# The down-projection of a two-layer encoder in two groups of channel pairs, with every sum on VectorE

## The chip, the cores and the metric

The kernel runs on one core of a Trainium2 chip. A core has TensorE (PE: matmuls; PEld: its weight loads), VectorE (DVE), ScalarE (ACT), GpSimd (POOL) and SyncE (SP, which issues the transfers here), each with an instruction queue of its own that it works through in order. They share the on-chip memory SBUF; matmuls add up in PSUM banks. The metric is the device time of one execution in microseconds, the median of several runs. Beside the runs one execution was recorded by the profiler; its rows are shown below.

## The reference, cut to what matters

Two layers, each an attention mix and a gated MLP. The change lies in the second matmul of the MLP, `@ w_down`, and in the normalisation and residual sum behind it:

```python
def conv_gated_mlp(h, w_up, conv_w, conv_b, w_down):
    u = h @ w_up
    ...                      # depthwise convolution of width 3 over the tokens: c
    gate, val = jnp.split(c, 2, axis=-1)
    return (jax.nn.gelu(gate, approximate=True) * val) @ w_down     # 1024 x 2816 times 2816 x 1024
...
    h = rms_norm(x, ffn_pre_gain[l])
    y = conv_gated_mlp(h, w_up[l], conv_w[l], conv_b[l], w_down[l])
    x = x + rms_norm(y, ffn_post_gain[l])                           # the input of the next layer, or the output
```

All is float32 at the interface.

## The kernel before

A float32 matmul is made of three (`mm3`, lines 255 to 257): each operand is cast to a rounded high half (hi) and a remainder (lo), and the products hi x hi, hi x lo and lo x hi are summed.

`gated` (first MLP matmul) works over 22 chunks j of 128 channels. It writes each gated chunk to a DRAM buffer, `self.gate[j]`. Its weights rotate over buffers (`slot`), some of which are slices of a shared place, "more".

`down` (second matmul) takes the 22 chunks as 11 pairs. For each pair it does a 2 x 2 block product with seven half-size products for eight (P1 to P7, in the order P2, P1, P5, P6, P3, P7, P4). One product of one pair is four token tiles of three matmuls, 12 matmuls of 128x512. A pair's eight pieces of 128x512 (four of the gated chunks, four of `w_down`) are loaded into a place of SBUF, `r`, whose pieces are numbered 0 to 7. `prep` makes the operands of a product: sums or differences of pieces (L1509), the cast of both operands to hi on ACT (L1528, named dhP), and the subtraction that gives lo on DVE (L1529, dlP). hi and lo rotate over 12 buffers ("whl", "raw", "rg"), so six products can be prepared ahead at most.

The pairs come in groups. `places` lists the places that each group's pairs use: 0 to 3 are the shared places (`share`), "fx" is one more place in a pool that is opened when the gated stage's buffers are done. All pairs of a group go through P2, then all through P1, and so on, in blocks of two pairs for each token tile. When a product of a group is complete, `add` brings it from PSUM into y (rows named yfK, yfQ, yfV): in group 0 the first piece of each y is an ACT copy, the others are sums on DVE (L1582). One-bank results go through the banks "ob", "pb" and others, two-bank results (named dx) through `ps2`.

The order on all engines comes from `self.at(t, f)`: f is due at time t (`st` = 2.73 is one product), and `emit` calls all of them sorted by t. A `prep` is due `DL` products ahead of its product. Pieces of later groups are loaded `DD` products ahead, or as soon as the place's last use is over (`free`).

`tail(t, T)` finishes a token tile: load the residual row xf, square and reciprocal root (ACT, POOL), multiply by the gain (`leave`, L303, on DVE or POOL), add into xf (L309), store. In layer 0 it also normalises for the next layer and transposes the row through PSUM (`split`, L274, pt_f; each half is cast by ACT at L275 and subtracted by DVE at L276).

Of the kernel before, what the change touches and what calls it, by code (L numbers as in the profile page):

```python
# [44 lines left out]
def r32(ap):  # L45
# [25 lines left out]
    DL=4, DD=12, DA=-0.02, DW=-10, DX=7.6, EM=1.5, EX=4.59, ES=5.89)  # L71
# [3 lines left out]
class Kernel:  # L75
# [1184 lines left out]
    def gated(self, l, ops, rows):  # L1260
# [5 lines left out]
        with tc.tile_pool(name=f"fu{l}", bufs=1, reuse_waits="tile") as pool:  # L1266
# [20 lines left out]
            def slot(name):  # L1287
                x = slots[n[0] % len(slots)]
                n[0] += 1
                if isinstance(x, str):  # L1290
                    return self.wp.tile([128, D], F32R, tag=x, name=name, bufs=slots.count(x))
                return extra["more"][:, x]

            def weights(j):
# [7 lines left out]
                q = self.wp.tile([128, NK, 128], F32, tag="qs", name=f"sums{l}_{j}")  # L1302

# [167 lines left out]
    def down(self, l, x_src, x_dst):  # L1471
# [7 lines left out]
        places = [(1, 2, 3), ("fx", 0, 1, 2, 3), ("fx", 0, 1)]  # L1479
        operands = dict(P1=(2, 6), P2=(0, 4), P3=(0, 5), P4=(1, 4), P5=None, P6=(2, 6), P7=(3, 7))  # L1480
# [23 lines left out]
        def prep(n, nm, p, tags):  # L1504

            r, tag = pairs[p]["r"], f"{nm}{l}_{p}"

            def tt(eng, out, a, b, op=ALU.subtract):
                eng.tensor_tensor(out=out, in0=a, in1=b, op=op)  # L1509

            if nm == "P5":
                q = pairs[p]["q"] = x["pool"].tile([128, 2, 512], F32, tag="q", name=f"q{tag}", bufs=5)
                tt(nc.vector, q[:, 0], r[:, 3], r[:, 1], ALU.add)
                tt(nc.vector, q[:, 1], r[:, 7], r[:, 6])
            if nm == "P6":
                q = pairs[p]["q"]
                tt(nc.gpsimd, r[:, 3::4], r[:, 2:6:3], r[:, 3::4])
                tt(nc.vector, r[:, 2], q[:, 0], r[:, 2])
                tt(nc.vector, r[:, 6], r[:, 5], q[:, 1])
            if nm == "P5":  # L1520
                src = pairs[p]["q"]
            else:
                a, b = operands[nm]
                src = r[:, a:b + 1:b - a]
            hi, lo = (x["pool" if t in ("rg", "q") else "wp"].tile([128, 2, 512], F32R, tag=t, name=f"d{e}{tag}",
                                                                 bufs=dict(whl=6, raw=2, rg=4, q=5)[t])
                      for e, t in zip("hl", tags))
            nc.scalar.copy(hi, src)  # L1528
# [35 lines left out]
        def add(nm, t, g):  # L1564
# [19 lines left out]
        gain, nh, pool_ = [], [], []  # L1584
# [4 lines left out]
        def tail(t, T):  # L1589
# [61 lines left out]
        for g, pl in enumerate(places):  # L1651
# [3 lines left out]
            for m, nm in enumerate(order):  # L1655
# [3 lines left out]
                if g == 2 and nm in ("P3", "P4"):  # L1659
                    blocks = [list(range(n))]  # L1660
                for b, ks in enumerate(blocks):
                    final = b == len(blocks) - 1
                    for k in ks:
                        tags = [slots[i % 12] for i in (2 * s, 2 * s + 1)]
                        if g == 2 and nm == "P7":
                            tags = [("rg", "rg"), ("q", "q"), ("q", "q")][k]
                        if g == 2 and nm == "P4":
                            tags = ("whl", "whl") if k == 2 else ("rg", "rg")
                        t = (s - P["DL"]) * st
                        self.at(t, lambda s=s, nm=nm, p=p0 + k, tags=tags: prep(s, nm, p, tags))  # L1670
# [118 lines left out]
```

## Time and profile before

| | |
|---|---|
| median of 3 runs | 2734.23 us (2732.19 to 2738.07) |
| the profiled execution | 2732.83 us |
| its span, first to last instruction | 2731.1 us |
| mean granted clock of TensorE | 0.984 of full speed |
| busy: PE / DVE / ACT / POOL | 2569.6 / 2173.0 / 1465.5 / 937.8 us |
| the same as shares of the span | 94% / 80% / 54% / 34% |
| down-projection, layer 0 | 1131.46 to 1361.3, then transposes to 1393.5 |
| down-projection, layer 1 | 2488.0 to 2716.9, then the last tiles to 2731.1 |

Shares are averages over stages that differ. The windows below cut the down-projection into stretches: a stretch in which PE is busy all the time runs at PE's own pace, and one where PE is busy for less than its length waits for something. A row of windows has the stretch, its length, the busy time of PE, PEld, DVE, ACT and POOL with the number of instructions, the granted TensorE clock, the busy share of the DMA engines and their GB/s. The clock is the granted TensorE clock: 1.00 is the upper of its two levels (2.4 GHz), 0.5 the lower (1.2 GHz), and numbers between are mixtures over the stretch. A timeline row has the start, the length and the engine, and in brackets how long the engine was idle before and for what.

### The profile page before, as it was taken

The numbers are of one execution on the slowest core, as the hardware profiler recorded it, in microseconds if no ns is written. First come the engines' busy times: TensorE is split into PE (matmuls) and PEld (weight loads), VectorE is DVE, ScalarE is ACT, GpSimd is POOL, SyncE is SP. The second block draws the span as 40 slices with busy tenths as digits, with TensorE's granted clock in tenths as the row PEclk, the third lists the DMA queues.
The fourth block names the chain that finished last, engine by engine and source line by source line (L and its number), as shares of the span: only waits on it lengthen the run. The fifth ranks groups of instructions, "written<-read, shape, count | busy, mean of one in ns | idle before, by whom it ended". The sixth has DMA issues, their size and how long they took to land. (4 is left out here: it accounts for less than half of the span.)

```text
span 2731.1 us, 40409 instructions
## 1 busy us (share of the span) xinstructions
PE 2569.6 (94%) x14533; PEld 2208.2 (81%) x14533; DVE 2173.0 (80%) x3117; ACT 1465.5 (54%) x2704; POOL 937.8 (34%) x808
## 2 busy tenths in 40 slices
PE   8999999996899999989989999999968999998997
PEld 7999888885788888777789998888757888886876
DVE  5347899989878878797864568999897888878978
ACT  5247677666544444443553467776655444454433
POOL 1343212264333434241233442113733333332413
PEclk9999999999999999999999999999989999999999
DMA  6343412234222222622252434122432222216222
GB/s 194 101 128 88 106 49 69 57 90 148 78 70 93 77 77 78 212 89 93 94 161 85 125 96 92 48 70 62 105 123 81 82 84 79 83 65 223 77 93 100
DMA packets 316916, 268.02 MB, mean 98 GB/s; under 512 B 104763, under 2 KB 262571, under 8 KB 316715
## 3 DMA queue, kind: packets, MB, share of 16 engines
q1 hardware_dynamic: 316714, 265.43, 32.4%
q8 instruction: 114, 1.87, 0.3%
q14 instruction: 88, 0.71, 0.1%
HBM read 183.30 MB, written 69.48 MB: 93 GB/s over the span
## 5 line engine op out<-in xcount | busy, mean ns | idle before, releaser
L1305 POOL TENSOR_TENSOR sums<-loads 128x512 f32<-128x512 f32 x84 | 169.8, 2021 | 153.1 <-DMA loads<-in_w_up 67.2
L1528 ACT CAST dhP<-rows 128x1024 fp32r<-128x1024 f32 x108 | 110.7, 1051 | 171.8 <-PE dx L257 63.9
L1529 DVE TENSOR_TENSOR dlP<-rows,dhP 128x1024 fp32r<-128x1024 f32 x108 | 160.6, 1513 | 35.8 <-ACT dhP L1528 35.7
L1305 POOL TENSOR_TENSOR loads<-loads,sums 128x512 f32<-128x512 f32 x42 | 57.8, 1377 | 371.2 <-DVE wgl L1315 229.7
L1509 POOL TENSOR_TENSOR rows<-rows 128x1024 f32<-128x1024 f32 x36 | 109.4, 3044 | 169.8 <-DVE qP L1509 42.8
L256 PE MATMUL dx<-dlP,dhP 128*128 128x512 f32 x328 | 130.4, 398 | 12.8 <-DVE dlP L1529 12.8
L255 PE MATMUL dx<-dhP 128*128 128x512 f32 x328 | 130.2, 397 | 9.5 <-ACT dhP L1528 5.4
L257 PE MATMUL dx<-dhP,dlP 128*128 128x512 f32 x328 | 129.6, 395 | 0.0
L1188 ACT CAST PTh_b<-pt_b 128x512 fp32r<-128x512 f32 x128 | 74.9, 588 | 57.9 <-PE pt_b L1183 56.9
L1373 DVE SCALAR_TENSOR_TENSOR c<-ug,cw,c 128x1023 f32<-128x1023 f32 x44 | 56.8, 1290 | 56.2 <-ACT c L1372 56.2
L1372 ACT ACTIVATE c<-ug,cw 128x1024 f32<-128x1024 f32 x44 | 54.7, 1243 | 85.7 <-DMA gate<-c 82.7
L255 PE MATMUL pb_mix<-whi_wa,h 128*128 128x256 f32 x320 | 100.0, 313 | 0.1
L255 PE MATMUL ux<-fT,wqh 128*128 128x512 f32 (+1 forms) x256 | 96.7, 378 | 1.3 <-ACT fT L275 1.3
L256 PE MATMUL ux<-fT,wqh 128*128 128x512 f32 (+1 forms) x256 | 96.5, 377 | 0.0
L257 PE MATMUL ux<-fT,wql 128*128 128x512 f32 (+1 forms) x256 | 96.3, 376 | 0.0
L1415 ACT ACTIVATE c<-c 128x1024 f32<-128x1024 f32 x44 | 46.7, 1062 | 86.5 <-DVE c L1375 86.5
L1193 DVE TENSOR_TENSOR PTl_c<-pt_c,PTh_c 128x512 fp32r<-128x512 f32 x128 | 85.5, 682 | 8.5 <-ACT PTh_c L1188 7.9
L1193 DVE TENSOR_TENSOR PTl_b<-pt_b,PTh_b 128x512 fp32r<-128x512 f32 x128 | 87.0, 683 | 6.2 <-ACT PTh_b L1188 5.4
L1028 PE MATMUL s_b<-rK,rQ 128*128 128x512 f32 x256 | 91.5, 414 | 0.4 <-ACT P_b L1105 0.4
L1188 ACT CAST PTh_c<-pt_c 128x512 fp32r<-128x512 f32 x128 | 74.5, 587 | 32.1 <-PE pt_c L1183 30.4
L256 PE MATMUL pb_mix<-wlo_wa,h 128*128 128x256 f32 x320 | 90.3, 282 | 0.0
L257 PE MATMUL pb_mix<-whi_wa,h 128*128 128x256 f32 x320 | 90.3, 282 | 0.0
(613 smaller groups left out, 9716.2 us busy)
## 6 DMA issues: line engine op xcount, KB each, us to landing
loads<-in_w_up SPq DMA_DIRECT2D x84, 512.0 KB
gate<-c SPq DMA_DIRECT2D x44, 512.0 KB
rows<-gate SPq DMA_DIRECT2D x72, 256.0 KB
rows<-in_w_down SPq DMA_DIRECT2D x72, 256.0 KB
z<-z SPq DMA_DIRECT2D x28, 512.0 KB
rK<-rK SPq DMA_DIRECT2D x48, 256.0 KB
xs<-xo SPq DMA_DIRECT2D x16, 512.0 KB
xf<-xs SPq DMA_DIRECT2D x16, 512.0 KB
```

The source lines that it names most:

```text
L255: nc.tensor.matmul(out, ah, bh, start=start and i == 0, stop=False, **flags)
L256: nc.tensor.matmul(out, ah, bl, start=False, stop=False, **flags)
L257: last = nc.tensor.matmul(out, al, bh, start=False, stop=stop and i == n - 1, **flags)
L1028: nc.tensor.matmul(out[:, c:c + w], Q[:, qt * 128:(qt + 1) * 128], K[:, k0 + c:k0 + c + w], start=i == 0, stop=i == len(ops) - 1)
L1188: nc.scalar.copy(x["sp"][0][:np, :n], x["pt"][:np, :n])
L1193: nc.vector.tensor_tensor(out=x["sp"][1][:np, :n], in0=x["pt"][:np, :n], in1=r32(x["sp"][0][:np, :n]), op=ALU.subtract)
L1305: nc.gpsimd.tensor_tensor(out=out, in0=a, in1=b, op=op)
L1372: nc.scalar.activation(c, u, AF.Identity, bias=b, scale=w1)
L1373: nc.vector.scalar_tensor_tensor(out=c[:, 1:], in0=u[:, :S - 1], scalar=w0, in1=c[:, 1:], op0=ALU.mult, op1=ALU.add)
L1509: eng.tensor_tensor(out=out, in0=a, in1=b, op=op)
L1528: nc.scalar.copy(hi, src)
L1529: nc.vector.tensor_tensor(out=lo, in0=src, in1=r32(hi), op=ALU.subtract)
```

## The change

Two groups, of 5 and 6 pairs, replace three of 3, 5 and 3. A second extra place "fy" joins "fx". The operands of all seven products are formed in place in `r` by DVE alone, a sum when its product comes up (P5, P6, P3, P7) or behind P1's subtraction; the copies "q" and POOL's sums are gone. Group 0's first two products put hi and lo into place 0, which group 0 leaves free (`first`); the last five P4 put them into places whose pairs are done (`dead`).

```diff
-    DL=4, DD=12, DA=-0.02, DW=-10, DX=7.6, EM=1.5, EX=4.59, ES=5.89)
+    DL=3, DD=14, DG=(0, 2), DA=-0.02, DW=-10, DX=7.6, EM=1.5, EX=4.59, ES=5.89)
...
-        places = [(1, 2, 3), ("fx", 0, 1, 2, 3), ("fx", 0, 1)]
-        operands = dict(P1=(2, 6), P2=(0, 4), P3=(0, 5), P4=(1, 4), P5=None, P6=(2, 6), P7=(3, 7))
+        places = [(1, 2, 3, "fx", "fy"), (0, 1, 2, 3, "fx", "fy")]
+        operands = dict(P1=(2, 6), P2=(0, 4), P3=(0, 5), P4=(1, 4), P5=(3, 6), P6=(3, 6), P7=(2, 7))
...
+        def tt(out, a, b, op=ALU.subtract):
+            nc.vector.tensor_tensor(out=out, in0=a, in1=b, op=op)
+
+        def prep(s, nm, p, where):
 
             r, tag = pairs[p]["r"], f"{nm}{l}_{p}"
-
-            def tt(eng, out, a, b, op=ALU.subtract):
-                eng.tensor_tensor(out=out, in0=a, in1=b, op=op)
-
             if nm == "P5":
-                q = pairs[p]["q"] = x["pool"].tile([128, 2, 512], F32, tag="q", name=f"q{tag}", bufs=5)
-                tt(nc.vector, q[:, 0], r[:, 3], r[:, 1], ALU.add)
-                tt(nc.vector, q[:, 1], r[:, 7], r[:, 6])
+                tt(r[:, 3], r[:, 3], r[:, 1], ALU.add)
             if nm == "P6":
-                q = pairs[p]["q"]
-                tt(nc.gpsimd, r[:, 3::4], r[:, 2:6:3], r[:, 3::4])
-                tt(nc.vector, r[:, 2], q[:, 0], r[:, 2])
-                tt(nc.vector, r[:, 6], r[:, 5], q[:, 1])
-            if nm == "P5":
-                src = pairs[p]["q"]
+                tt(r[:, 3:7:3], r[:, 1:6:4], r[:, 2:7:4])
+            if nm == "P3":
+                tt(r[:, 0:5:4], r[:, 0:5:4], r[:, 3:7:3])
+            if nm == "P7":
+                tt(r[:, 7], r[:, 5], r[:, 7])
+            a, b = operands[nm]
+            src = r[:, a:b + 1:b - a]
+            if where is None:
+                hi, lo = ((self.wp if t != "rg" else x["pool"]).tile(
+                    [128, 2, 512], F32R, tag=t, name=f"d{e}{tag}", bufs=dict(whl=6, raw=2, rg=4)[t])
+                    for e, t in zip("hl", (slots[i % 12] for i in (2 * s, 2 * s + 1))))
             else:
-                a, b = operands[nm]
-                src = r[:, a:b + 1:b - a]
-            hi, lo = (x["pool" if t in ("rg", "q") else "wp"].tile([128, 2, 512], F32R, tag=t, name=f"d{e}{tag}",
-                                                                 bufs=dict(whl=6, raw=2, rg=4, q=5)[t])
-                      for e, t in zip("hl", tags))
+                hi, lo = where()
             nc.scalar.copy(hi, src)
             nc.vector.tensor_tensor(out=lo, in0=src, in1=r32(hi), op=ALU.subtract)
             ring[nm, p] = hi, lo
-            if nm == "P6":
-                tt(nc.gpsimd, r[:, 0::4], r[:, 0::4], r[:, 2::4])
+            if nm == "P1":
+                tt(r[:, 2:7:4], r[:, 2:8:5], r[:, 3:7:3])
+        def first(n):
+
+            if "first" not in x:
+                x["first"] = self.share(0, F32R, f"first{l}", (8, 512))
+            return [x["first"][:, 4 * n + e:4 * n + e + 2] for e in (0, 2)]
+
+        def dead(i, n):
+
+            if ("late", i) not in x:
+                x["late", i] = self.share(i, F32R, f"late{l}_{i}", (8, 512)) if i != "fx" else x["pool"].tile(
+                    [128, 8, 512], F32R, tag=i, name=f"late{l}_{i}")
+            return [x["late", i][:, 4 * n + e:4 * n + e + 2] for e in (0, 2)]
```

The P4 of group 1 goes in two blocks of three pairs, in layer 0 it adds onto banks of the P7 before it, and the transposes of tiles 0 to 3 come at due times of their own. All residual rows use three buffers, "z". The loads of group 0 have a new order: place 1 first, "fx" and "fy" from the moment that the gated stage is over.

```diff
-            if nm in ("P1", "P6", "P7") or nm == "P4" and g < 2:
+            if nm in ("P1", "P6", "P7") or nm == "P4" and not (g and last):
...
-                x["xt"] = self.load_x((self.wp, "z", 3) if t < 4 else (pool_[0], "q", 5), x_src, t, f"xf{l}_{t}")
+                x["xt"] = self.load_x((self.wp, "z", 3), x_src, t, f"xf{l}_{t}")
...
-                x["rs"] = self.square(junk(), y[t], f"p{tag}", y[t], gain[0], nc.vector if t % 2 or last and t > 4 else None)
+                x["rs"] = self.square(junk(), y[t], f"p{tag}", y[t], gain[0], None if t in P["DG"] and not last or t == 4 else nc.vector)
...
-                       (P["DX"] + P["ES"] if t > 3 else end - T + .05 - (1.5 - .5 * min(t, 3)) * st, split)]
+                       (P["DX"] + P["ES"] if t > 3 else 18 + 1.3 * t, split)]
...
-                if g == 2 and nm in ("P3", "P4"):
-                    blocks = [list(range(n))]
+                if g and nm == "P4":
+                    blocks = [[0, 1, 2], [3, 4, 5]]
...
+                        elif g and nm == "P4" and k:
+
+                            where = lambda k=k: dead(pl[(0, 0, 1, 1, 4)[k - 1]], (0, 1, 0, 1, 0)[k - 1])
+                        t = (s - P["DL"]) * st + .05
+                        self.at(t, lambda s=s, nm=nm, p=p0 + k, where=where: prep(s, nm, p, where))
...
             for k, i in enumerate(pl):
-                for a, nm, done in ((0, "P2", "P3"), (4, "P2", "P4"), (2, "P1", "P6"), (6, "P1", "P6"), (1, "P5", "P4"),
-                                   (3, "P5", "P7"), (5, "P6", "P3"), (7, "P5", "P7")):
+                for a, nm, done in ((0, "P2", "P3"), (4, "P2", "P4"), (2, "P1", "P7"), (6, "P1", "P3"), (3, "P1", "P3"),
+                                    (7, "P1", "P7"), (1, "P5", "P4"), (5, "P6", "P7")):
                     t = use[k, nm]
-                    t = max(free.get((i, a), -1e9) + .01, t - P["DD"] * st) if g else -100 + t
-                    assert not g or t < use[k, nm] - st
+                    if g:
+                        t = max(free.get((i, a), -1e9) + .02, t - P["DD"] * st)
+                        assert t < use[k, nm] - 3 * st, (k, i, a, (use[k, nm] - t) / st)
+                    elif isinstance(i, int):
+                        t -= 100 + 50 * (i == 1)
+                    else:
+                        t = max(0, t - 6 * st) + .0001 * t * (t > 0)
```

In `gated`, the weights of the last chunk skip the slices of "more" (place 0), since `first` takes that place (`slot` calls itself until the turn of another buffer).

Three places where instructions move. In names, dlP60_1 is the lo of P6, layer 0, pair 1; rows0_2 is the place 2 of layer 0; c0_21 and uv0_21 belong to chunk 21 of the gated stage; the last number of a name only counts tiles.

First, DVE's queue in group 0 of layer 0 between the operands of P5 and those of P6. Before (POOL's sums stand in its own queue; the pairs of 512-wide sums into rows0_2 and rows0_3 are DVE's part of P6):

```order
L1529 TENSOR_TENSOR dlP50_2_12011<-qP50_2_12007,dhP50_2_12010 128x1024
L1582 TENSOR_TENSOR yfK0_11964<-yfK0_11964,dx0_0_0_11980 128x2x512
L1529 TENSOR_TENSOR dlP60_0_12030<-rows0_1_11785,dhP60_0_12029 128x1024
L1582 TENSOR_TENSOR yfK0_11964<-yfK0_11964,dx0_0_2_12000 128x2x512
L1509 TENSOR_TENSOR rows0_2_11788<-qP50_1_11987,rows0_2_11788 128x512
L1509 TENSOR_TENSOR rows0_2_11788<-rows0_2_11788,qP50_1_11987 128x512
L1509 TENSOR_TENSOR rows0_3_11791<-qP50_2_12007,rows0_3_11791 128x512
L1509 TENSOR_TENSOR rows0_3_11791<-rows0_3_11791,qP50_2_12007 128x512
```

After:

```order
L1509 TENSOR_TENSOR rows0_1_11787<-rows0_1_11787 128x2x512
L1509 TENSOR_TENSOR rows0_2_11796<-rows0_2_11796 128x2x512
L1509 TENSOR_TENSOR rows0_3_11799<-rows0_3_11799 128x2x512
L1531 TENSOR_TENSOR dlP50_3_12121<-rows0_fx_11921,dhP50_3_12120 128x1024
L1597 TENSOR_TENSOR yfK0_12006<-yfK0_12006,dx0_0_0_12022 128x2x512
L1597 TENSOR_TENSOR yfK0_12006<-yfK0_12006,dx0_0_2_12041 128x2x512
L1531 TENSOR_TENSOR dlP50_4_12140<-rows0_fy_11924,dhP50_4_12139 128x1024
L1531 TENSOR_TENSOR dlP60_0_12158<-rows0_1_11787,dhP60_0_12157 128x1024
L1509 TENSOR_TENSOR rows0_fx_11921<-rows0_fx_11921 128x2x512
L1509 TENSOR_TENSOR rows0_fy_11924<-rows0_fy_11924 128x2x512
L1531 TENSOR_TENSOR dlP60_1_12175<-rows0_2_11796,dhP60_1_12174 128x1024
```

A pair's sum for P6 is one instruction of 128x2x512 in place, and those of three pairs stand together ahead of the subtractions that use them.

Second, DVE's queue across the start of the down-projection, where the convolution of chunk 21 is still to be done. Before:

```order
L1373 SCALAR_TENSOR_TENSOR c0_21_0_11868<-ug0_21_0_11812,cw_520,c0_21_0_11868 128x1023
L1375 SCALAR_TENSOR_TENSOR c0_21_0_11868<-ug0_21_0_11812,cw_520,c0_21_0_11868 128x1023
L1529 TENSOR_TENSOR dlP20_2_11882<-rows0_3_11791,dhP20_2_11881 128x1024
L1529 TENSOR_TENSOR dlP10_0_11886<-rows0_1_11785,dhP10_0_11885 128x1024
L1529 TENSOR_TENSOR dlP10_1_11927<-rows0_2_11788,dhP10_1_11926 128x1024
L1373 SCALAR_TENSOR_TENSOR c0_21_1_11902<-uv0_21_0_11866,cw_520,c0_21_1_11902 128x1023
L1529 TENSOR_TENSOR dlP10_2_11944<-rows0_3_11791,dhP10_2_11943 128x1024
L1375 SCALAR_TENSOR_TENSOR c0_21_1_11902<-uv0_21_0_11866,cw_520,c0_21_1_11902 128x1023
```

After:

```order
L1377 SCALAR_TENSOR_TENSOR c0_21_0_11870<-ug0_21_0_11814,cw_520,c0_21_0_11870 128x1023
L1509 TENSOR_TENSOR rows0_2_11796<-rows0_2_11796 128x512
L1379 SCALAR_TENSOR_TENSOR c0_21_0_11870<-ug0_21_0_11814,cw_520,c0_21_0_11870 128x1023
L1531 TENSOR_TENSOR dlP10_2_12001<-rows0_3_11799,dhP10_2_12000 128x1024
L1509 TENSOR_TENSOR rows0_2_11796<-rows0_2_11796 128x512
L1509 TENSOR_TENSOR rows0_3_11799<-rows0_3_11799 128x2x512
L1377 SCALAR_TENSOR_TENSOR c0_21_1_11897<-uv0_21_0_11868,cw_520,c0_21_1_11897 128x1023
L1531 TENSOR_TENSOR dlP20_3_11932<-rows0_fx_11921,dhP20_3_11931 128x1024
L1379 SCALAR_TENSOR_TENSOR c0_21_1_11897<-uv0_21_0_11868,cw_520,c0_21_1_11897 128x1023
```

Ahead of the subtraction for pair 3 of P2 (dlP20_3) now stand sums and a subtraction for P1 among the convolution's steps; pairs 3 and 4 belong to group 0 now.

Third, PE's queue at the transposes of tile 1 in layer 0. Before, they lie behind the last P4 product, among the next layer's projection (ob_mix1 with weights whi_wd1):

```order
L257 MATMUL dx0_2_p4_13457<-dhP40_10_13340,dlP40_10_13341 128x512
L255 MATMUL ob_mix1_11914<-whi_wd1_0_0_13381,h1_20_13467 128x256
L256 MATMUL ob_mix1_11914<-wlo_wd1_0_0_13382,h1_20_13467 128x256
L274 MATMUL pt_f20_1_0_13494<-idf_87,yfK0_11964 128x128 x4
L257 MATMUL ob_mix1_11914<-whi_wd1_0_0_13381,h1_21_13468 128x256
```

After, they lie in the first block of P4:

```order
L255 MATMUL dx0_1_0_12700<-dhP40_5_13247 128x512
L256 MATMUL dx0_1_0_12700<-dlP40_5_13248,dhP40_5_13247 128x512
L274 MATMUL pt_f20_1_0_13325<-idf_87,yfK0_12006 128x128 x4
L257 MATMUL dx0_1_0_12700<-dhP40_5_13247,dlP40_5_13248 128x512
L274 MATMUL pt_f20_1_4_13332<-idf_87,yfK0_12006 128x128 x4
```

Those of tiles 0, 2 and 3 are moved likewise, tile 0 into P7's last block; those of tiles 4 to 7 stay behind P4.

## Rows read from the trace of the kernel before

**Rows 1.** Windows, layer 0: us, busy by engine (instructions), clock, DMA, GB/s
```profile
1148.50:1175.00 26.50, 16.12 (x53) 11.46 (x52) 26.50 (x20) 9.18 (x11) 14.99 (x5) 0.74 0.28 91
1175.00:1284.00 109.00, 109.00 (x482) 90.24 (x481) 90.69 (x84) 44.48 (x44) 31.20 (x10) 1.00 0.27 90
1284.00:1291.00 7.00, 4.78 (x20) 3.33 (x20) 7.00 (x7) 3.04 (x3) 3.79 (x2) 1.00 0.22 76
...
1342.00:1361.30 19.30, 18.31 (x83) 14.30 (x81) 16.99 (x19) 15.18 (x29) 7.31 (x7) 1.00 0.76 245
1361.30:1393.50 32.20, 21.86 (x142) 19.78 (x142) 25.48 (x38) 27.79 (x56) 12.97 (x13) 0.89 0.47 163
```

**Rows 2.** Windows, layer 1, columns as in rows 1
```profile
2505.00:2530.00 25.00, 14.31 (x49) 10.15 (x48) 25.00 (x20) 9.19 (x11) 14.01 (x6) 0.80 0.27 92
...
2640.00:2647.00 7.00, 5.04 (x22) 3.52 (x21) 7.00 (x7) 3.05 (x3) 4.16 (x2) 1.00 0.23 75
...
2698.00:2717.00 19.00, 17.09 (x73) 13.17 (x71) 18.51 (x18) 6.12 (x12) 6.58 (x5) 1.00 0.61 215
2717.00:2731.10 14.10, 0.00 (x0) 0.00 (x0) 10.47 (x9) 4.09 (x11) 7.22 (x6) 0.65 0.39 157
```

**Rows 3.** Waits of PE, 1100 to 1400: total us, times, longest
```profile
PE dx L256 <- DVE dlP L1529: 6.2, 2, 5.9
PE pt_f L274 <- DVE h L276: 5.9, 5, 2.7
PE pt_f L274 <- ACT yfV L1633: 3.0, 1, 3.0
PE dx L255 <- ACT dhP L1528: 2.7, 1, 2.7
PE ob_mix L256 <- DVE dlP L1529: 2.4, 2, 1.4
PE dx L255 <- DVE yfQ L1582: 1.6, 1, 1.6
```

**Rows 4.** Timeline of DVE in layer 0: start us, us
```profile
1142.81 3.43 DVE L1529 TENSOR_TENSOR dlP<-qP,dhP 128x1024 fp32r<-128x1024 f32 x1
...
1148.97 1.21 DVE L1529 TENSOR_TENSOR dlP<-qP,dhP 128x1024 fp32r<-128x1024 f32 x1
1150.10 0.68 DVE L1509 TENSOR_TENSOR qP<-rows 128x512 f32<-128x512 f32 x1
...
1151.31 2.88 DVE L1509 TENSOR_TENSOR rows<-rows,qP 128x512 f32<-128x512 f32 x1
```

**Rows 5.** Timeline of POOL, the same stretch
```profile
1141.82 6.67 POOL L1509 TENSOR_TENSOR rows<-rows 128x1024 f32<-128x1024 f32 x2 [41.45 <-DMA rows<-in_w_down]
1150.91 2.72 POOL L1509 TENSOR_TENSOR rows<-rows 128x1024 f32<-128x1024 f32 x1 [2.42 <-issue]
```

**Rows 6.** Instructions of lines 1509 and 1529: ns min/median/max, first and last start
```profile
L1509 POOL TENSOR_TENSOR rows<-rows x36: 2376/3174/5504, 1141.8 to 2672.7; 128x1024 f32<-128x1024 f32 x36
...
L1529 DVE TENSOR_TENSOR dlP<-rows,dhP x108: 1209/1219/3431, 1110.7 to 2706.6; 128x1024 fp32r<-128x1024 f32 x108
```

**Rows 7.** Lines of DVE by form, layer 0: busy us, mean ns
```profile
L1582 DVE TENSOR_TENSOR yfK<-yfK,dx 128x1024 f32<-128x1024 f32 x10 | 12.0, 1208 | 0.0
```

**Rows 8.** Timeline of DVE before the stage's start
```profile
1129.82 1.28 DVE L1373 SCALAR_TENSOR_TENSOR c<-ug,cw,c 128x1023 f32<-128x1023 f32 x1 [1.30 <-ACT c L1372]
```

**Rows 9.** Windows around the start, columns as in rows 1
```profile
1135.00:1145.00 10.00, 10.00 (x46) 8.29 (x45) 10.00 (x10) 5.74 (x8) 3.18 (x1) 1.00 1.01 354
```

**Rows 10.** Timeline of SP's queue: first load into the extra place
```profile
1131.66 0.33 SPq L1500 DMA_DIRECT2D rows_fx<-gate  x1
```

**Rows 11.** Timeline of the end of layer 1
```profile
2718.10 2.72 DVE L303 TENSOR_TENSOR yfQ<-yfQ,g_ff 128x1024 f32<-128x1024 f32 x1
...
2726.20 1.27 DVE L309 SCALAR_TENSOR_TENSOR xf<-yfV,rs_pf,xf 128x1024 f32<-128x1024 f32 x1
```

**Rows 12.** Lines of ACT, layer 0: busy us, mean ns
```profile
L1528 ACT CAST dhP<-rows 128x1024 fp32r<-128x1024 f32 x50 | 51.2, 1050 | 75.7 <-PE dx L257 32.3 <-PE dz_P L257 23.3 <-issue 8.8
```

More of the change, by code (lines that the diff above doesn't have):

```diff
@@ L1289, in slot @@
                 n[0] += 1
+                if extra.get("last") and not isinstance(x, str):
+                    return slot(name)
                 if isinstance(x, str):
@@ L1302, in weights @@
                 q = self.wp.tile([128, NK, 128], F32, tag="qs", name=f"sums{l}_{j}")
+                extra["last"] = j == NFF - 1
                 def tt(out, a, b, op):
@@ L1488, in place @@
             if i not in raw:
-                raw[i] = self.share(i, F32, f"rows{l}_{i}", (8, 512)) if i != "fx" else x["pool"].tile(
-                    [128, 8, 512], F32, tag="fx", name=f"rows{l}_fx")
+                raw[i] = self.share(i, F32, f"rows{l}_{i}", (8, 512)) if isinstance(i, int) else x["pool"].tile(
+                    [128, 8, 512], F32, tag=i, name=f"rows{l}_{i}")
             return raw[i]
@@ L1568, in add @@
             half, cols = dict(P2=(0, 0), P1=(0, 0), P5=(1, 1), P6=(0, 1), P3=(0, 1), P7=(1, 1), P4=(1, 0))[nm]
-            two = nm in ("P1", "P6", "P7") or nm == "P4" and (g < 2 or t > 1)
+            two = nm in ("P1", "P6", "P7") or nm == "P4" and (not (g and last) or t > 1)
             if two and t % 2 == 0:
                 return
-            for c in (1, 0) if nm == "P7" and g == 2 else (cols,):
+            for c in (1, 0) if nm == "P7" and g and last else (cols,):
                 c = slice(c * 512, c * 512 + 512)
                 if two:
-                    ps = (x["p4"] if nm == "P4" and g == 2 else x["x", g, t // 2]).rearrange("p (a b) -> p a b", b=512)
+                    ps = (x["p4"] if nm == "P4" and g and last else x["x", g, t // 2]).rearrange("p (a b) -> p a b", b=512)
                     out = x["y"][2 * half + t // 2][:, :, c]
@@ L1582, in add @@
                     added[t + 4 * half] = added[t - two + 4 * half] = nc.vector.tensor_tensor(out=out, in0=out, in1=ps, op=ALU.add)
-        gain, nh, pool_ = [], [], []
+        gain, nh = [], []
         def gains():
@@ L1663, in down @@
                     for k in ks:
[L1664 to L1670, printed above, removed]
+                        where = None
+                        if s < 2:
+                            where = lambda s=s: first(s)
+                        elif g and nm == "P4" and k:
+                            where = lambda k=k: dead(pl[(0, 0, 1, 1, 4)[k - 1]], (0, 1, 0, 1, 0)[k - 1])
+                        t = (s - P["DL"]) * st + .05
+                        self.at(t, lambda s=s, nm=nm, p=p0 + k, where=where: prep(s, nm, p, where))
                         use[k, nm] = t
@@ L1673, in down @@
                     for t in range(4):
-                        first, fin = b == 0 and (nm in ("P2", "P1", "P5") or nm == "P4" and g == 2), final
-                        self.at(ts, lambda nm=nm, t=t, g=g, ks=ks, p0=p0, first=first, fin=fin: product(
+                        first_, fin = bool(b == 0 and (nm in ("P2", "P1", "P5") or nm == "P4" and g and last)), final
+                        self.at(ts, lambda nm=nm, t=t, g=g, ks=ks, p0=p0, first=first_, fin=fin: product(
                             nm, bank(nm, t, g), [p0 + k for k in ks], t, first, fin))
@@ L1680, in down @@
                             self.at(ts + P["DA"], lambda nm=nm, t=t, g=g: add(nm, t, g))
-                            if g == 2 and nm in ("P3", "P4"):
-                                tail(4 * half + t, ts + (nm == "P4" and t == 2) * n * st / 4)
+                            if g and nm in ("P3", "P4"):
+                                tail(4 * half + t, ts + (nm == "P4" and t % 2 == 0 and (t == 2 or not last)) * len(ks) * st / 4)
             for k, i in enumerate(pl):
-                for a, nm, done in ((0, "P2", "P3"), (4, "P2", "P4"), (2, "P1", "P6"), (6, "P1", "P6"), (1, "P5", "P4"),
-                                   (3, "P5", "P7"), (5, "P6", "P3"), (7, "P5", "P7")):
+                for a, nm, done in ((0, "P2", "P3"), (4, "P2", "P4"), (2, "P1", "P7"), (6, "P1", "P3"), (3, "P1", "P3"),
+                                    (7, "P1", "P7"), (1, "P5", "P4"), (5, "P6", "P7")):
                     t = use[k, nm]
-                    t = max(free.get((i, a), -1e9) + .01, t - P["DD"] * st) if g else -100 + t
-                    assert not g or t < use[k, nm] - st
+                    if g:
[5 more added lines that the diff above has]
+                        t = max(0, t - 6 * st) + .0001 * t * (t > 0)
                     self.at(t, lambda p=p0 + k, i=i, a=a: load(p, i, a, a + 1))
@@ L1702, in rest @@
                 x["pool"] = pool
-                pool_.append(pool)
                 self.emit()
```

1 line of the change is left out of this document (removed).

## The prediction, made before the changed kernel was run

> **What bounds the kernel now.** I read the stages of the down-projection first, because the change lies in it alone. In layer 0 it starts at 1131.46 and its last product ends at 1361.3. One clean stretch gives TensorE's own pace: 482 matmuls in 109.00 us without idle time at clock 1.00, 0.2261 us each [rows 1]. A product of one pair is 12 matmuls, 2.71 us, and the stage has 77: 208.9 us. The other stages hold fewer matmuls than their length allows. From 1148.50 there are 53 in 26.50 us, so 26.50 - 53 x 0.2261 = 14.5 us are lost, partly idle and partly at clock 0.74; from 1284.00, 7.00 - 20 x 0.2261 = 2.5; from 1342.00, 19.30 - 83 x 0.2261 = 0.5 [rows 1]. That is 17.5 us. Layer 1 repeats it: 25.00 - 49 x 0.2261 = 13.9, 7.00 - 22 x 0.2261 = 2.0, 19.00 - 73 x 0.2261 = 2.5, together 18.4 us [rows 2]. (A missing matmul record would make a loss look 0.2 us too large.)
>
> Then the waits of TensorE: it waits for dlP, the low halves that VectorE subtracts (6.2 us in two waits, and 2.4 at the ob_mix bank), for the cast dhP (2.7) and for a sum into yfQ that frees a bank (1.6) [rows 3]. So VectorE is late, and in the 26.50 us it is busy all the time, with only 20 instructions [rows 1].
>
> The timelines tell why 20 instructions take 26 us. The subtraction at 1142.81 takes 3.43 us and the 512-wide sum at 1151.31 takes 2.88; the subtraction at 1148.97 takes 1.21 and the sum at 1150.10 takes 0.68 [rows 4]. The long ones lie beside POOL's sums: two from 1141.82 for 6.67 us, one at 1150.91 for 2.72 [rows 5]. Both read SBUF with two inputs. Over the kernel the median subtraction is 1.219 us and the longest 3.431, the median POOL sum 3.174 and the longest 5.504 [rows 6]. VectorE's sums out of PSUM stay at 1.208 us on average [rows 7].
>
> The Trainium skill ("SBUF — State Buffer", section "Who interferes with whom") says that VectorE and GpSimd contend for one shared pair of ports, and that it is held as an exclusive lock for a whole instruction. The trace agrees: 3.43 us against 1.21, as if the other's sum had to end first. By that rule taking the sums off POOL removes the whole stretch; were it a sharing of bandwidth of which half stayed, 18 of the 36 us lost would stay too, and the time would be 2720.
>
> **The change, part by part.**
>
> 1. POOL's sums go to VectorE. 22 POOL sums per layer, two for each of 11 pairs, vanish, and their stretching with them. VectorE's own work per layer becomes 77 subtractions, 33 sums of 1024 and 22 of 512, and the sums out of PSUM: 8 pieces of 512 or 1024 in group 0 (the others are ACT copies) and 20 in group 1. Busy time: 77 x 1.21 + 33 x 1.21 + 22 x 0.68 + 12 x 1.21 + 16 x 0.68 = 173 us of 208.9, or 83%. Queued instructions start closer than they last (1148.97 to 1150.10 is 1.13 for one of 1.21 [rows 4]), which makes it about 160, 77%. The row for an in-place 1024-wide sum on VectorE does not exist. Its bounds are 1.13 (the pace of a subtraction of that size) and 2.88 (a stretched sum [rows 4]); I take 1.13, the row of the same shape, since nothing on POOL stands beside it any longer outside the tails; at 2.88 VectorE would be the bound (first rival).
>
> 2. Three groups become two. Group 0 has five pairs for three, so VectorE's and ACT's start-up is spread over 5 products at each stage. The stages in which work is tight are P1, P6 and P3 of group 1: six subtractions and six sums of 1024, 12 x 1.13 = 13.6, and four 512 or two 1024 sums out of PSUM, 2.4: 16.0 us beside 72 x 0.2261 = 16.3 of TensorE. They are full, but the other four stages are light (P2: 6 x 1.13 = 6.8 of 16.3), and the preparation is queued three products, 8.1 us, ahead. Cost zero, covered by those 8.1 us. If the cover went, each 0.1 us per product over 2.71 would cost 18 x 0.1 a layer. One round of sums into y vanishes (about 16 us of VectorE), off the path.
>
> So 17.5 and 18.4 go. What comes instead:
>
> 3. The start. Group 0 wants five pairs of rows, and VectorE's queue now holds three sums and two subtractions of group 0 between the last channels' convolution. From the convolution step at 1129.82 [rows 8]: steps 1.20, sum 0.60, step 1.20, subtraction 1.13, sums 0.60 and 1.13, step 1.20, subtraction of the fourth pair 1.21 gives 1138.1. TensorE wants that one after 28 matmuls, 1131.46 + 6.3 = 1137.8. That is 0.3 late. The rows for the fourth and fifth pair come over DMA engines that are 101% busy at 354 GB/s [rows 9], so it may be more; the two new places overlie buffers of the gated stage that its last channel has read before the down-projection starts, while the first load into the old extra place was issued only at 1131.66 [rows 10], after it, so they are no later than that. I take 1.5 per layer, bounds 0 and 4 (the four rows of 256 KB that P2 needs of those two pairs last 3 us at 354 GB/s).
>
> 4. The end of layer 0. The transposes of tiles 0 to 3 move from behind P4 into P7's last block and P4's first. They take PE no more time than before, but each pair of them must be cast by ACT and subtracted by VectorE before the banks come free, and in both queues stand P4's own casts and the tails of tiles 0 to 3. Now these waits cost 5.9 and 3.0 [rows 3]. I take 5 in the products, bounds 1 and 9. In exchange only tiles 4 to 7 are left after the last product. That stretch is 32.20 us with PE busy 21.86, clock 0.89 [rows 1]: 10.3 idle and some 3.5 of slow clock. I take 5 of these 13.8 back, bounds 0 and 9.
>
> 5. The end of layer 1. P4 in two blocks of three pairs: VectorE's tail sums come between; I take 1.5, bounds 0 and 3. Then 14.10 us are left after the last matmul [rows 2], in which a VectorE multiply of 1024 lasts 2.72 beside POOL's (2718.10 [rows 11]); the change leaves POOL one multiply there, and the chain ends with the sum at 2726.20. I take 1 back, bounds 0 and 2. The input tiles now share three buffers, so tile 7's load waits for tile 4's store; the two 512 KB transfers would still end about when that sum can run.
>
> Nothing else on SP's or POOL's queue is moved past a step that TensorE waits for; the skipped weight slots at the last channel cost nothing, as the buffers of channel 20 are by then read.
>
> **Sum.** Layer 0: -17.5 + 1.5 + 5 - 5 = -16.0. Layer 1: -18.4 + 1.5 + 1.5 - 1 = -16.4. Together -32.4. The profiled execution took 2732.83 (span 2731.1), so 2700.4. The median of the runs is 2734.23, 1.4 above, so 2701.8: I say 2702.
>
> **The rivals.**
>
> *VectorE becomes the bound (slower).* In the 33 products a layer of P1, P6 and P3 the sum is in place: it waits for the subtraction and the cast before it, and the cast after waits for it. If these go one after the other, a product takes 1.21 + 1.05 + 1.21 = 3.47 us ([rows 6, 12]) for 2.71: 0.76 x 66 = 50 us over both layers against 32.4, of which the lead of 8.1 us may hide as much in each layer. Without it +18, 2752; with half of it +10, 2744, the time I give it. (At 2.88 per sum the same mechanism takes 4.01 per product and 86 us, 2788.) It decides from 0.5 us per product (32.4/66). For it: 98% in these stages. Against it: the queue alternates pairs, so one pair's cast lies beside another's sum, and in the clean stretch VectorE was busy 90.69 of 109.00 us with no idle of PE [rows 1]. 0.09.
>
> The Trainium skill ("Perfetto Trace Analysis", section "Optimizing Scalar/DVE Operations") advises the opposite direction, moving work off a saturated VectorE to Scalar or even GpSimd, and adds that between these two it might not help since they share a port. The stretched rows here bear out the second half.
>
> *The end of layer 0 takes more.* If transposes, tails and late casts wait on each other in turns, 9 instead of 5 in the products and 0 instead of 5 after them, with 3 for 1.5 and 0 for 1 in layer 1: 4 + 5 + 1.5 + 1 = 11.5 more, 2713. For it: transposes wait there six times now, each time for another engine [rows 3]. Against: half of VectorE's load is gone. 0.18.
>
> *All stalls go.* Start 0.3, transposes 1, 7 of 13.8 back, layer 1 without loss: 1.2 x 2 + 4 + 2 + 1.5 less, 2692. 0.12.
>
> *The waits stay.* TensorE waits for rows, not for VectorE: then the 6.2 and 2.7 stay at the new group's P1 or P5, the clock falls as before, and only the 2.5 and 2.0 at the later groups go: 2730, no change. Against: 20 instructions fill VectorE's 26.50 us without a gap [rows 1], so it did not wait for data. 0.06.
>
> **How the numbers follow.** Forecast 0.55, the others 0.09, 0.18, 0.12, 0.06. The likeliest case alone spans 2694 to 2711 by its bounds (start 0 to 4 a layer, end of layer 0 plus or minus 5). The range 2688 to 2721 takes in the forecast, the costly end and the clean one, 0.85 in all, and leaves out the slower and the unchanged case. A difference of 0.2% (5.5 us) is what a measurement of this kernel can tell from none. Faster 0.86 (forecast, the costly end, the clean one and a bit of the fourth), same 0.05, slower 0.09.
>
> **What would show it.** Right: no VectorE instruction of the down-projection above 1.4 us outside the tails, no stretch of slow clock in P5 and P6 of group 0, PE idle in the body below 3 us a layer, VectorE's busy time down to about 160 to 175 us a layer. Wrong: waits of dx or ob_mix for dlP in P6 and P3 of group 1 (VectorE the bound), waits for rows from SP's loads at the start, pt_f waits over 9 us in P4, or sums of 1024 above 1.3 us.

## The result, and the profile after

The changed kernel takes 2693.05 us (median of 4 runs, 2688.35 to 2696.92) against 2733.21 for the kernel before on the same chip: a ratio of 0.9849, 95% interval 0.9829 to 0.987. That is 40 us; in two later sets of runs (c1 and c2 below) the same kernel gave 0.9827 [0.9812, 0.9842] and 0.9837 [0.9823, 0.985]. Forecast were 2702 and 32 us.

Windows of the profile after, layer 0, columns as in [rows 1], from the stage's start at 1129.55; the second to the fourth are cut at the same times as there, though the stage starts 1.9 us earlier:

```profile
1129.50:1148.50 19.00, 18.20 (x80) 14.74 (x80) 19.00 (x20) 9.74 (x13) 0.00 (x0) 1.00 0.87 302
1148.50:1175.00 26.50, 26.50 (x118) 21.95 (x118) 26.43 (x25) 12.89 (x15) 0.00 (x0) 1.00 0.45 163
1175.00:1284.00 109.00, 109.00 (x483) 90.28 (x482) 83.39 (x84) 44.15 (x44) 0.00 (x0) 1.00 0.25 82
1284.00:1291.00 7.00, 7.00 (x33) 5.79 (x32) 6.79 (x8) 2.31 (x3) 0.00 (x0) 1.00 0.00 1
...
1322.00:1348.10 26.10, 22.60 (x114) 18.09 (x113) 21.00 (x29) 20.45 (x37) 3.65 (x4) 1.00 0.66 186
1348.10:1373.00 24.90, 22.04 (x168) 20.74 (x166) 17.71 (x26) 18.74 (x41) 10.45 (x12) 1.00 0.66 208
```

The window of 26.50 us that held 53 matmuls [rows 1] now holds 118, at clock 1.00. VectorE is still busy in it, but with 25 instructions, and PE does not wait for it. 18.20 of the first 19.00 us are busy: that is the one stall left at the start. Layer 1:

```profile
2469.00:2486.00 17.00, 16.92 (x75) 13.66 (x75) 17.00 (x17) 9.61 (x12) 0.00 (x0) 1.00 0.89 310
2486.00:2511.00 25.00, 25.00 (x112) 20.71 (x111) 24.94 (x24) 11.70 (x14) 0.00 (x0) 1.00 0.46 160
...
2621.00:2628.00 7.00, 7.00 (x32) 5.79 (x32) 7.00 (x8) 2.00 (x2) 0.00 (x0) 1.00 0.01 2
...
2662.00:2679.80 17.80, 17.36 (x76) 13.68 (x74) 11.26 (x12) 5.83 (x11) 3.42 (x3) 1.00 0.20 65
2679.80:2692.40 12.60, 0.00 (x0) 0.00 (x0) 8.29 (x9) 2.36 (x6) 2.13 (x3) 0.59 0.57 209
```

Waits of PE from 1090 to 1390, and the subtractions and sums of the down-projection (ns min/median/max), which answer to [rows 3, 6]:

```profile
PE ob_mix L255 <- ACT jkf L300: 2.0, 1, 2.0
PE pt_f L274 <- DVE h L276: 1.8, 1, 1.8
PE dx L255 <- DVE yfQ L1597: 1.1, 1, 1.1
PE ob_mix L256 <- DVE dlP L1531: 0.8, 1, 0.8
...
```

```profile
L1531 DVE TENSOR_TENSOR dlP<-rows,dhP x88: 1210/1218/1226, 1123.0 to 2656.5; 128x1024 fp32r<-128x1024 f32 x88
...
L1531 DVE TENSOR_TENSOR dlP<-rows_fx,dhP x26: 1212/1218/3356, 1135.6 to 2653.1; 128x1024 fp32r<-128x1024 f32 x26
```

The longest is no longer 3431 but 1226 ns, with one exception of 3356: it starts at 1311.98, beside a multiplication by the gain that POOL still does (from 1311.85). The in-place sums, 512-wide ones among them, have their median at 1214 ns and their longest at 1222:

```profile
L1509 DVE TENSOR_TENSOR rows<-rows x70: 678/1214/1222, 1126.5 to 2633.7; 128x1024 f32<-128x1024 f32 x42, 128x512 f32<-128x512 f32 x28
```

**Where the 38.7 us of the two profiled spans (2731.1 and 2692.4) lie.** A landmark that both kernels pass behind layer 0's end is the last pt_cq transpose of layer 1 (before, then after):

```profile
L274 PE MATMUL pt_cq<-idf,cqn x24: 270/272/333, 1404.1 to 1521.0; 128*128 128x128 f32 x24
```

```profile
L274 PE MATMUL pt_cq<-idf,cqn x24: 270/271/272, 1378.7 to 1497.4; 128*128 128x128 f32 x24
```

From the stage's start: 1521.0 - 1131.46 = 389.5 against 1497.4 - 1129.55 = 367.9, so layer 0 gives 21.7 (predicted 16.0). Layer 1's products take 2679.8 - 2469.0 = 210.8 for 228.9, 18.1 (predicted 15.4), and what follows them 12.6 for 14.2, 1.6 (predicted 1). The code ahead of the stage ran 1.9 shorter, and that between 1497.4 and layer 1's down-projection at 2469.04 took 971.6 for 967.0, 4.6 longer. Both stretches are the same code.

Most of the 4.6 is the clock. Windows of this profile, and the same windows in the profile of a later run of the same kernel:

```profile
1525.00:1535.00 10.00, 8.53 (x53) 8.09 (x52) 3.31 (x14) 4.77 (x12) 1.40 (x2) 0.83 0.38 119
1940.00:1950.00 10.00, 8.29 (x43) 7.12 (x42) 6.32 (x15) 4.25 (x12) 6.25 (x8) 0.83 0.78 280
```

```profile
1525.00:1535.00 10.00, 9.03 (x69) 8.56 (x68) 3.45 (x15) 6.09 (x16) 1.90 (x3) 1.00 0.49 156
1940.00:1950.00 10.00, 7.86 (x49) 6.64 (x47) 7.92 (x18) 4.23 (x12) 6.83 (x8) 1.00 0.82 305
```

A clock of 0.83 is a short stay on the lower level; the second execution has none in these windows, and there the whole stretch takes 966.6 us. Matmul by matmul, the two executions part by 1.9 us in the first window and by 1.7 in the second; another 1.3 is a wait for ACT at 2229.88 (1.53 us here, 0.20 there), at clock 1.00 in both. So the 4.6 do not belong to the change, and are part of why single runs scatter over 8 us.

### The profile page after: what moved, and what is told of

Read it like the earlier page. It is cut to its first block, busy times and chain, and to the rows that moved or that the text cites. A ratio compares the mean times of both kernels' runs of the same rounds, so it can differ in the third digit from the quotient of the medians.

```text
span 2692.4 us, 40234 instructions
## 1 busy us (share of the span) xinstructions
PE 2565.2 (95%) x14533; PEld 2210.0 (82%) x14533; DVE 2111.1 (78%) x3099; ACT 1463.6 (54%) x2704; POOL 798.2 (30%) x761
## 5 line engine op out<-in xcount | busy, mean ns | idle before, releaser
L1530 ACT CAST dhP<-rows 128x1024 fp32r<-128x1024 f32 x88 | 89.4, 1052 | 130.1 <-issue 53.7
L86 POOL TENSOR_TENSOR rs_pf<-rs_pf,mhalf 128x1 f32<-128x1 f32 x15 | 13.9, 928 | 467.7 <-ACT rs_pf L85 467.6
L1531 DVE TENSOR_TENSOR dlP<-rows,dhP 128x1024 fp32r<-128x1024 f32 x88 | 105.2, 1219 | 40.7 <-ACT dhP L1530 40.7
L255 PE MATMUL dx<-dhP 128*128 128x512 f32 x308 | 120.2, 390 | 1.1 <-DVE yfQ L1597 1.1
L257 PE MATMUL dx<-dhP,dlP 128*128 128x512 f32 x308 | 120.0, 389 | 0.0
L256 PE MATMUL dx<-dlP,dhP 128*128 128x512 f32 x308 | 119.8, 389 | 0.0
L257 PE MATMUL ux<-fT,wql 128*128 128x512 f32 (+1 forms) x272 | 102.6, 377 | 0.0
```

The lines of the kernel that those rows point to most:

```text
L255: nc.tensor.matmul(out, ah, bh, start=start and i == 0, stop=False, **flags)
L256: nc.tensor.matmul(out, ah, bl, start=False, stop=False, **flags)
L257: last = nc.tensor.matmul(out, al, bh, start=False, stop=stop and i == n - 1, **flags)
```

## The experiments

**The sums alone (e1), and that kernel with the gains too (e10).** The kernel before, with

```diff
-                tt(nc.gpsimd, r[:, 3::4], r[:, 2:6:3], r[:, 3::4])
+                tt(nc.vector, r[:, 3::4], r[:, 2:6:3], r[:, 3::4])
...
-                tt(nc.gpsimd, r[:, 0::4], r[:, 0::4], r[:, 2::4])
+                tt(nc.vector, r[:, 0::4], r[:, 0::4], r[:, 2::4])
```

> The kernel before with one difference: its two POOL sums per pair run on VectorE, groups and all else as before. Contention theory (POOL's sums stretch VectorE's SBUF instructions): VectorE gets 22 x 1.13 = 25 us more work a layer but loses about 35 us of stretch; no VectorE instruction above 1.4 us in P5 and P6 of group 0; the 26.5 us window shrinks by 4 to 8 us a layer, in all 10 to 20 us faster than before, 2713 to 2723. Group theory (the gain comes from five pairs in group 0 and the new order, not from the engine): nothing gained or, with the additional work on the late engine, 0 to 10 slower, 2733 to 2743.

Measured: 2700.92 us, ratio 0.9871 [0.9853, 0.9889]; a second time (e11) 2700.19, 0.9885 [0.9869, 0.9902]. 33 us of the 40 come from these two words, more than the 10 to 20 expected for contention, and nothing of the group theory is left for them. The expectation counted VectorE's shortened window and left out that the slow clock goes with the wait: a window of 26 us around the start of P5 (1148.4 in this run) holds 109 matmuls at clock 1.00, where 53 in 26.50 us were [rows 1].

```profile
1146.00:1172.00 26.00, 24.82 (x109) 19.90 (x108) 25.96 (x28) 14.79 (x17) 0.00 (x0) 1.00 0.47 152
```

Its waits at the end of layer 0 are those of [rows 3]:

```profile
PE pt_f L274 <- DVE h L276: 5.9, 5, 2.7
PE pt_f L274 <- ACT yfV L1633: 3.0, 1, 3.0
```

**The sums given back (e2).** The changed kernel, with the in-place sums of P6 and P3 on POOL:

```diff
-            if nm == "P6":
-                tt(r[:, 3:7:3], r[:, 1:6:4], r[:, 2:7:4])
-            if nm == "P3":
-                tt(r[:, 0:5:4], r[:, 0:5:4], r[:, 3:7:3])
...
+            if nm == "P5":
+                nc.gpsimd.tensor_tensor(out=r[:, 3:7:3], in0=r[:, 1:6:4], in1=r[:, 2:7:4], op=ALU.subtract)
+            if nm == "P6":
+                nc.gpsimd.tensor_tensor(out=r[:, 0:5:4], in0=r[:, 0:5:4], in1=r[:, 3:7:3], op=ALU.subtract)
```

> The changed kernel with the sums for P6 and P3 (two per pair, 22 a layer, as many as before) given back to POOL, each issued as early as its inputs allow (behind the preparation of P5 and P6). Contention theory: VectorE's 1024-wide instructions reach 3.4 us beside them and TensorE waits again in P6 and P3, 10 to 35 us slower than the changed kernel, 2703 to 2728. Group theory: VectorE has 25 us less of its own work a layer, so no slower than 2693 plus or minus 5.

Measured: 2729.1 us, 0.9976 [0.9966, 0.9986], 36 slower than the changed kernel, though VectorE has 22 sums a layer fewer to do. VectorE's subtractions reach 3.4 us again, and PE waits for them in layer 0:

```profile
L1527 DVE TENSOR_TENSOR dlP<-rows,dhP x88: 1210/1218/3426, 1124.4 to 2688.7; 128x1024 fp32r<-128x1024 f32 x88
```

```profile
PE dx L256 <- DVE dlP L1527: 8.2, 2, 6.6
PE ob_mix L256 <- DVE dlP L1527: 7.0, 3, 5.3
```

This could still be a wait for POOL's results: ACT's casts do wait for these sums here, 21.9 us in five waits in layer 0. The next two separate that.

**POOL busy for nobody (e3, e4).** Behind each preparation of P5 and P6, with `q` a tile that no other engine reads. The one-column instruction reads lo, so that POOL starts when lo is done. e3:

```diff
...
+                q, one = x["dum"], r32(lo)[:, 0, 0:1]
+                nc.gpsimd.tensor_tensor(out=q[:, 0, 0:1], in0=one, in1=one, op=ALU.subtract)
+                nc.gpsimd.tensor_tensor(out=q, in0=q, in1=q, op=ALU.subtract)
```

e4 has, in the place of the last line:

```diff
+                nc.gpsimd.memset(q, 0.0)
+                nc.gpsimd.memset(q, 0.0)
```

> The changed kernel, plus on POOL one subtraction of 128x1024 from SBUF to SBUF behind each preparation of P5 and P6 (22 a layer), on a tile of its own that nobody reads, each started by a one-column instruction that waits for that product's lo. Contention theory: though nobody waits for POOL, VectorE's subtractions and sums beside it reach 3.4 us, its work rises from 160 towards 200 us a layer and TensorE waits; 10 to 50 us slower than the changed kernel, 2703 to 2743. Wait theory (before, VectorE and TensorE were late because they waited for the results of POOL's slow sums): no change, 2693 plus or minus 5.

> As the run with POOL's additional subtractions, but two memsets of 128x1024 on POOL in the place of each subtraction: POOL is busy at the same places and writes SBUF, but reads nothing. If it is POOL's reading that blocks VectorE: VectorE's instructions stay at 1.21 and 0.68 us, 2693 plus or minus 5. If any work of POOL on SBUF blocks it: stretched instructions and a time as in the run with the subtractions, in proportion to POOL's busy time.

Measured: e3 2735.71 us, 1.0003 [0.9992, 1.0014]; the whole gain is gone. e4 2691.05, 0.9834 [0.9818, 0.9851], no loss. The instructions of e3 (VectorE, then POOL), and of e4:

```profile
L1531 DVE TENSOR_TENSOR dlP<-rows_fy,dhP x26: 1207/1214/2893, 1136.7 to 2694.2; 128x1024 fp32r<-128x1024 f32 x26
```

```profile
L1541 POOL TENSOR_TENSOR dum<-dum x44: 1893/2757/2761, 1150.7 to 2661.5; 128x1024 f32<-128x1024 f32 x44
```

```profile
L1531 DVE TENSOR_TENSOR dlP<-rows_fy,dhP x26: 1210/1216/1226, 1138.9 to 2652.2; 128x1024 fp32r<-128x1024 f32 x26
```

```profile
L1541 POOL MEMSET dum<- x44: 952/956/966, 1152.9 to 2629.2; 128x1024 f32 x44
```

The wait theory has fallen: in e3 nobody needs a result of POOL, and VectorE is stretched as before. One wait is left: ACT's casts wait 5.4 us in all for the one-column instruction to have read lo; e4 has that wait too, 9.2 us, and loses nothing. It is not POOL's being busy either: two memsets of 0.956 us stretch nothing, and POOL is busy for 943.6 us in e4 and 968.2 in e3. The VectorE timeline of e3 shows which of its instructions suffer:

```profile
1158.42 1.21 DVE L1531 TENSOR_TENSOR dlP<-rows_fx,dhP 128x1024 fp32r<-128x1024 f32 x1
1159.55 2.34 DVE L1604 TENSOR_TENSOR yfK<-yfK,dx 128x1024 f32<-128x1024 f32 x2
1161.82 2.89 DVE L1531 TENSOR_TENSOR dlP<-rows_fy,dhP 128x1024 fp32r<-128x1024 f32 x1
```

The two sums out of PSUM at 1159.55 (2.34 us for two) lie beside a POOL subtraction that runs from 1158.62 for 2.76 us, and are not stretched; in the whole of e3 no sum out of PSUM takes more than 1.222 us. The subtraction with two SBUF inputs at 1161.82 is stretched: it lies beside POOL's from 1161.73 to 1163.62, and ends 1.1 us after that one, about its own length. The Trainium skill ("SBUF — State Buffer", section "SBUF: two separate sides") says just this: a VectorE instruction with two SBUF inputs contends with GpSimd only where that one reads SBUF, and whoever starts first holds the ports for its whole instruction. The rows agree with each part: 2.89 us behind POOL's subtraction in e3, at most 1.226 for the subtractions from fy beside the memsets of e4, and the sums out of PSUM not stretched. That it is POOL's reading, and not another difference between a memset and a subtraction, these runs do not separate.

**The end of layer 0 (e5, e6, e8, e10).** The transposes' old due time in the changed kernel, and its gains without POOL (`DG=()` and no exception for t = 4):

> The changed kernel with the transposes of tiles 0 to 3 of layer 0 due where they were before: in and behind the last of P4 instead of in P7's last block and P4's first. The prediction's terms (5 us lost in the products, 5 won behind them) say no difference, 2693 plus or minus 4. If the move is worth what the trace suggests (10.3 us of idle PE behind the products fell to 2.9, and the clock stayed at 1.00 there): 6 to 10 slower than the changed kernel, 2699 to 2703.

> The changed kernel with the last multiplications by the gain on POOL (tiles 0, 2 and 4) moved to VectorE too. Contention theory: the last stretched subtraction (3.36 us at the start of P4's tails) falls to 1.21 and VectorE's wait of 2.1 us for POOL's product goes; up to 4 us faster, 2689 to 2693. Rival: VectorE is the fuller engine in the tails, 3 multiplies of 1.21 on its path, up to 3 us slower, 2693 to 2696.

> The changed kernel itself, unchanged, on the same chip as the other runs of this call: 2693 plus or minus 3. Its profile shows whether the four short stretches of half clock in the attention of layer 1 (about 4 us of the gain given back there) belong to the change or come and go between executions: if they come and go, this profile has them elsewhere or not at all.

Measured on one chip: e5 2686.43, 0.9822 [0.9805, 0.9838]; e6 2684.24, 0.9813 [0.9799, 0.9828]; the changed kernel (c1) 2688.07. So moving the transposes was worth nothing, and the other expectation, 6 to 10, is wrong. The gains on VectorE look 4 us better; once more:

> The changed kernel itself once more, as the partner of the next two runs on one chip: 2688 to 2693.

> The changed kernel with every multiplication by the gain on VectorE, once more with more rounds. If the 3.8 us between it and the changed kernel are real: 3 to 5 us under the partner run. If they are scatter: within 1.5 us of it.

> The changed kernel with the gains on VectorE and the transposes of tiles 0 to 3 late. If the two edits are independent (3.8 and 1.6 us by their runs): 5 us under the partner run. If the early transposes and POOL's multiplications were one stall (each waits for the other's tile): no better than the run with the gains alone.

c2 2689.75 (2685.15 to 2692.17), e9 2684.09 (2682.06 to 2686.96), ratio 0.9822 [0.9808, 0.9835], e8 2685.92, 0.9824 [0.9811, 0.9837]. Twice 4 to 6 us under its partner, with intervals of the ratios that overlap. The profiles place it: what follows layer 1's products takes 11.5 us in e6, e8 and e9 and 12.6 to 12.7 in the three profiles of the changed kernel, and layer 0, from the stage's start to the last pt_cq transpose, 360.3 to 363.1 against 367.3 to 368.0. So the version with all gains on VectorE is probably better than the changed kernel by a few us; by the times alone that is at the edge of what was measured. The late transposes add nothing to it.

e10 is e1 with the gains on VectorE as well (`nc.vector` for every tile in `leave`):

> The kernel before with its sums on VectorE, once more as the partner of the next run on one chip: 2701 plus or minus 3.

> The kernel before (three groups, its blocks and its transposes) with the sums and also all multiplications by the gain on VectorE. What is still 8 to 12 us between the kernel before with its sums on VectorE (2701) and the changed one (2688 to 2693) lies at the end of layer 0. If it is POOL's multiplications there (2.4 to 3.0 us each, on the way to the transposes): 4 to 8 under the partner, 2693 to 2697, and the wait of 3.0 us for the normalised row shrinks. If it is the new grouping (two blocks of three pairs, two-tile sums, longer stages over which the tails spread): no more than 2 under the partner, 2699 to 2701, with the 5.9 and 3.0 us waits of the transposes as before.

Measured: 2701.85 against 2700.19, no difference, and the transposes still wait:

```profile
PE pt_f L274 <- DVE h L276: 4.4, 2, 3.8
PE pt_f L274 <- ACT yfQ L1633: 3.0, 1, 3.0
PE pt_f L274 <- ACT yfV L1633: 2.0, 1, 2.0
```

So what is left between 2700 and 2688 to 2693 belongs to the rest of the change: the new grouping, its blocks, and what came with them. Which part of it (six pairs in the last group, P4 in two blocks, the two-tile sums, the order of the loads, the buffers of the residual rows) was not tried apart. Where it lies, the profiles of e1 and of the changed kernel show: layer 0's products take 213.9 and 218.7 us, what follows them up to the last pt_cq transpose 159.7 and 149.1, layer 1's products 213.8 and 210.7, the end 14.2 and 12.7. The rest of the change costs 4.8 us in layer 0's products and gains 10.5 behind them and 4.6 in layer 1.

## Why the prediction was right, and where its sizes were off

1. *POOL's sums stretch VectorE; without them the losses of 17.5 and 18.4 us go.* Shown, from three sides: removed in the old order (-33), put back in the new one (+36), put back without any result being used (+43). By windows the stall at P5 and P6 went whole: 118 matmuls in 26.50 us, 112 in 25.00 in layer 1.
2. *Two groups cost nothing; the full stages P1, P6, P3 are covered by the lead.* The windows of the body hold PE at 109.00 of 109.00 and 7.00 of 7.00 us. That it is the lead of three products which covers these stages is argued: no run shortens it. The rival in which VectorE becomes the bound did not happen: an in-place sum lasts 1.222 us at most (taken: 1.13 by pace, 1.21 busy). In that rival's bracket the cast was left out: 1.21 + 1.05 + 2.88 is 5.14 us a product and not 4.01. VectorE's busy time in the products fell from 203 and 207 us to 181 and 174; the sign named was 160 to 175, so layer 0 lies above it (third number behind the length):

```profile
1129.50:1348.10 218.60, 214.30 (x958) 176.53 (x958) 181.16 (x185) 109.21 (x140) 14.64 (x12) 1.00 0.35 117
2469.00:2679.80 210.80, 210.28 (x925) 173.09 (x924) 173.78 (x171) 91.64 (x107) 7.63 (x7) 1.00 0.32 110
```

3. *The start, 1.5 a layer.* About 0.9 in layer 0 (80 matmuls in the 18.95 us from the stage's start): the subtraction for the fourth pair runs at 1135.58 for 1.22 us, and PE waits 0.80 for it; layer 1 has none over 0.1 (16.92 of its first 17.00 us are busy). It is VectorE's queue, as worked out, and no row landed late: the part of the 1.5 that was set aside for late rows was not needed.

```profile
1135.58 1.22 DVE L1531 TENSOR_TENSOR dlP<-rows_fx,dhP 128x1024 fp32r<-128x1024 f32 x1
```

```profile
1136.85 0.50 PE L256 MATMUL ob_mix<-dlP,dhP 128*128 128x512 f32 x1 [0.80 <-DVE dlP L1531]
```

4. *The end of layer 0, +5 in the products and -5 behind them.* The second half is mis-sized, and is the largest part of the 9 us by which the forecast was too high. The products, from the stage's start to the end of the last one, take 218.7 us for 229.8: 11.1 shorter, where the terms give 17.5 - 1.5 - 5 = 11.0. From there to the last pt_cq transpose it is 149.1 for 159.7: 10.6 shorter, and not 5. Behind the products 24.90 - 22.04 = 2.9 us are idle, for 10.3, and the clock is 1.00, for 0.89 [rows 1], so more than 10 of the 13.8 came back. The cause given, that fewer transposes are left behind the products, is not it. In e5 48 of the 64 transposes lie behind the last product, for 32 in the changed kernel, and the stretch takes 148.6 us. Neither the sums nor POOL's multiplications do it in the old grouping: 159.7 in e1, 160.9 in e10. It comes with the new grouping, and by what mechanism stays open. (Before, eight transposes lay ahead of the end of the last product already, so 24 were moved and not 32.)
5. *The end of layer 1, +1.5 and -1.* In the last window PE is idle for 0.4 us (17.36 of 17.80 are busy), and the end is 1.6 shorter: right sign, some 2 us better together.

The rival "all stalls go" (2692, given 0.12) is the one that came nearest; the forecast's mechanism and sign were right, and the time lies in its range. The split behind it was not as forecast: the sums were to give 36 us and gave 33 by themselves, and the other terms were to cost 1.5 + 5 - 5 + 1.5 + 1.5 - 1 = 3.5 and gained 7 to 13 (e1 and e11 at 2700 to 2701, the changed kernel at 2688 to 2693). That gain was not foreseen.

## What to carry to other kernels

Before an element-wise sum of two SBUF operands is moved to POOL to relieve a busy VectorE, compare the longest and the median duration of VectorE's own instructions beside it. Here 22 POOL sums of about 3 us a layer cost VectorE more than doing them itself: its busy time over the kernel was 2173.0 us with them on POOL and 2147.4 when it did them too (e1), and the kernel took 33 us longer. Memsets on POOL did not have that price (e4), and VectorE's sums out of PSUM were not stretched beside POOL's subtractions (e3); so work that POOL takes over should only write, or lie where VectorE reads PSUM. A stall that ends in a lower clock is worth more than its idle time: count the matmuls in the stretch against the clean pace and not the gaps.

## What the runs showed of the hardware that was not expected

The blocking is mutual: in e3 the one-column POOL instruction takes 0.19 us beside VectorE's sums out of PSUM and 1.04 to 1.06 behind its subtractions and sums of two SBUF operands, and POOL's 1024-wide one takes 2.76 where such an instruction of VectorE is under way when it starts (1158.42 for 1.21) and 1.89 where POOL's starts first (1161.73, ahead of the subtraction at 1161.82).

```profile
1157.49 1.05 POOL L1540 TENSOR_TENSOR dum<-dlP 128x1 f32<-128x1 f32 x1
1158.62 2.76 POOL L1541 TENSOR_TENSOR dum<-dum 128x1024 f32<-128x1024 f32 x1
1161.46 0.19 POOL L1540 TENSOR_TENSOR dum<-dlP 128x1 f32<-128x1 f32 x1
1161.73 1.89 POOL L1541 TENSOR_TENSOR dum<-dum 128x1024 f32<-128x1024 f32 x1
```
